# Dilated and latent attention: the sum of a value product's two halves, and the masked product of the row sums, on GpSimd

## The chip, the cores and the metric

One core of a Trainium2 chip runs the whole program. The metric is device microseconds (us) of one execution. PE is TensorE, DVE is VectorE, ACT is ScalarE, POOL is GpSimd, SP is SyncE, which issues the DMAs.

## The reference

Two layers of an encoder, in float32, on a sequence of 1024 rows of 1024 numbers. Only the first layer's attention matters here. It has 8 heads of dilated windows (A) and 8 heads of latent attention (B), 64 wide each:

```python
# A: three windowed branches per head, mixed by the softmax of their log sums
p = jnp.exp(s - m); den = jnp.sum(p, -1)
o = jnp.einsum('bgnhqk,bgnkhd->bgnqhd', p, vw) / den
wts = jax.nn.softmax(jnp.stack(lses, 0), axis=0)
o = jnp.sum(wts[..., None] * jnp.stack(outs, 0), 0)
# B: plain softmax attention over all 1024 keys
s = jnp.einsum('bqhd,bkhd->bhqk', qblk, k) * scale
o = jnp.einsum('bhqk,bkhd->bqhd', jax.nn.softmax(s, -1), v)
```

The result of A and B, side by side, goes through one output projection; then come a feed-forward layer and the second layer.

## The kernel before

Products are made of two parts each, a rounded one and its rest (names that end in h and l), so that TensorE's fast float mode keeps float32's accuracy. A value tile V holds both parts of a head's 64 values side by side in 128 columns. The product of the weights with V therefore gives two half sums, one in PSUM partitions 0 to 63 and one in 64 to 127; they must be added. `halves` does that: ACT copies the half that lies in the wrong partitions out of PSUM into a temporary tile in SBUF (L790), and DVE adds the temporary to the other half, still in PSUM, into the destination (L792). The destination is `S_["s1"]` (the tile mixA), `S_["s2"]` (a part of the tile bX) or `S_["sB"]` (mixB). The temporaries are two tiles taken in turn: `hv` and another part of bX. The PSUM tile `m` has two buffers, shared with all other small products; `b`, for scores and transposes, has three.

Heads come in four pairs. A pair has 8 units of A (4 for each head: `part` 0 or 1, `g` 0 or 1) and 16 of B, and each unit passes three stages that are delayed against each other, so that several units are under way at once: scores (L735 for A, L83 to L85 for B), row minimum on DVE (L738, L823) and exponential on ACT (L745, L825); transposes on PE (L753, L830), whose result is split on ACT and DVE (L74 and L75: aPh and aPl, bPh and bPl); the product with V (L774, L846) and `halves`. `halves` runs after each unit of A and after every fourth unit of B, 48 times in this stage. The second layer's attention uses `halves` too, 16 times.

When a head starts, GpSimd copies its queries and keys in another order: aQ at L712, aK at L713, with one buffer each, so that these copies wait for the last product that reads the old ones. `pair_finish` ends a pair while the next one is under way: the row sums `st` are multiplied by a mask (fXe, L867) and brought into another order by a product; the factors are made; each result is multiplied by them (L922), and GpSimd adds s2 to s1 (L926, two instructions).

Each engine runs its instructions in the order that was fixed when the program was built, and waits in it for semaphores. That order is made by a scheduler from the whole program, so a change of some instructions can move others.

Of the kernel before, what the change touches and what calls it, by code (L numbers as in the profile page):

```python
# [9 lines left out]
AF = mybir.ActivationFunctionType  # L10
ALU = mybir.AluOpType
# [3 lines left out]
P = 128  # L15
# [17 lines left out]
class K:  # L33
# [665 lines left out]
    def dil_unit(self, S_, h, part, g):  # L699
        nc, wk, ps = self.nc, self.wk, self.ps  # L700
        hd = h % 2
        self.pair_state(S_)
        if ("a", h) not in S_:
            S_["a", h] = self.dil_load(h)
        Q, Kt, Bt, V1, V2 = S_["a", h]
        cls = "p l (j c) -> p l c j"
        Kc = S_.get(("k", h), Kt.rearrange(cls, c=4))
        Qc = S_.get(("q", h), Q.rearrange("p (j c) -> p c j", c=4))
        if self.inside and ("k", h) not in S_:
            Kc = S_["k", h] = self.t(wk, [P, 2, 4, 256], F32R, "aK", bufs=1)  # L710
            Qc = S_["q", h] = self.t(wk, [P, 4, 256], F32R, "aQ", bufs=1)
            nc.gpsimd.tensor_copy(Qc, Q.rearrange("p (j c) -> p c j", c=4))  # L712
            nc.gpsimd.tensor_copy(Kc, Kt.rearrange(cls, c=4))  # L713
        st = S_["A"]
        sp = self.t(ps, [P, 4, 256], F32, "b")
        sb = self.t(self.pHA, [P, 4, 256], F32, "aS", bufs=3)
        tiles, biases = [], []
        for tt in range(4):
            j0, j1 = 0, 256
            if part == 0:  # L720
                t = 4 * g + tt
                j0 = 64 if t == 0 else 0
                j1 = 192 if t == 7 else 256
                q = Q[:, t * P:(t + 1) * P]
                k = [Kt[:, l, 128 * t - 64 + j0:128 * t - 64 + j1] for l in range(2)]
                b0 = 64
            else:
                c, hf = 2 * g + tt // 2, tt % 2
                t = 4 * hf + c
                q = Qc[:, c, hf * P:(hf + 1) * P]  # L730
                k = [Kc[:, l, c] for l in range(2)]
                b0 = 128 - 128 * hf
            tiles.append((tt, t, j0, j1))
            for l in range(2):
                nc.tensor.matmul(sp[:, tt, j0:j1], lhsT=q, rhs=k[l], start=l == 0, stop=l == 1)  # L735
            biases.append(Bt[:, part, b0 + j0:b0 + j1])
        for (tt, t, j0, j1), bias in zip(tiles, biases):
            nc.vector.tensor_tensor_reduce(sb[:, tt, j0:j1], sp[:, tt, j0:j1], bias, 1.0, 3e38,  # L738
                                           ALU.add, ALU.min, st[:, part, 0, hd, t:t + 1])
            if j0 > 0:  # L740
                nc.gpsimd.memset(sb[:, tt, :j0], 0.0)
            if j1 < 256:
                nc.gpsimd.memset(sb[:, tt, j1:], 0.0)
        for tt, t, j0, j1 in tiles:
            nc.scalar.activation(sb[:, tt, j0:j1], sb[:, tt, j0:j1], AF.Exp, scale=-1.0,  # L745
                                 bias=st[:, part, 0, hd, t:t + 1], accum_out=st[:, part, 1, hd, t:t + 1])
        yield
        wk, ps = self.wk, self.ps
        tp = self.t(ps, [P, 8, P], F32, "b")
        for tt in range(4):  # L750
            for kc in range(2):
                pos = tt * 2 + kc if part == 0 else (tt // 2) * 4 + kc * 2 + tt % 2
                nc.tensor.transpose(tp[:, pos], sb[:, tt, kc * P:(kc + 1) * P], self.ident)  # L753
        pt = (self.t(wk, [P, 8, P], F32R, "aPh"), self.t(wk, [P, 8, P], F32R, "aPl"))
        self.split(pt[0], pt[1], tp)
        yield
        self.pair_sums(S_, h // 2)
        pv = self.t(ps, [P, 512], F32, "m", bufs=2)
        mms = []
        if part == 0:  # L760
            t0 = 4 * g
            for p0, n, ch in ((1, 2, t0), (5, 2, t0 + 2), (3, 2, t0 + 1), (0, 1, (t0 - 1) % 8), (7, 1, t0 + 3)):
                c0 = (p0 // 2) * P
                mms.append((pv[:, c0:c0 + n * P], V1[:, ch], slice(p0, p0 + n)))
        else:
            for cc in range(2):
                for kc in range(2):
                    p0 = cc * 4 + kc * 2
                    mms.append((pv[:, cc * 256:(cc + 1) * 256], V2[:, kc, 2 * g + cc], slice(p0, p0 + 2)))
        for i, (o, v, pp) in enumerate(mms):  # L770
            for l in range(2):
                first = (i == 0 if part == 0 else i % 2 == 0) and l == 0
                last = (i == 4 if part == 0 else i % 2 == 1) and l == 1
                nc.tensor.matmul(o, lhsT=v, rhs=pt[l][:, pp], start=first, stop=last)  # L774
        if part == 0:
            self.halves(S_["s1"][g], pv, hd)
        else:
            self.halves(S_["s2"][:, g * 512:(g + 1) * 512], pv, hd)
        yield

    def halves(self, dst, pv, hd):

        nc = self.nc
        mine, other = slice(64 * hd, 64 * hd + 64), slice(64 - 64 * hd, 128 - 64 * hd)
        if self.hv:
            self.hv.append(self.hv.pop(0))
            tmp = self.hv[0]
        else:
            tmp = self.t(self.wk, [P, 512], F32, "hv", bufs=2)
        nc.scalar.activation(tmp[mine], pv[other], AF.Copy)  # L790
        o, a, b = dst[mine], pv[mine], tmp[mine]
        nc.vector.tensor_tensor(o, a, b, ALU.add)  # L792

    def mla_load(self, wk, h):
        nc = self.nc
# [13 lines left out]
    def mla_unit(self, S_, h, t):  # L809
        nc, wk, ps = self.nc, self.wk, self.ps  # L810
        hd = h % 2
        self.pair_state(S_)
        if ("b", h) not in S_:
            S_["b", h] = self.mla_load(self.pHB, h)
        Q, Kt, V = S_["b", h]
        st = S_["B"]
        sp = self.t(ps, [P, S], F32, "b")
        q = [Q[:96, l, t * P:(t + 1) * P] for l in range(2)]
        for half in range(2):
            ks = slice(half * 512, half * 512 + 512)  # L820
            self.mm3(sp[:, ks], q, [Kt[:96, l, ks] for l in range(2)], True, True)
        pr = self.t(wk, [P, S], F32, "bP", bufs=3)
        nc.vector.tensor_tensor_reduce(pr, sp, self.zero.to_broadcast([P, S]), 1.0, 3e38, ALU.add, ALU.min,  # L823
                                       st[:, 0, hd, t:t + 1])
        nc.scalar.activation(pr, pr, AF.Exp, scale=-1.0, bias=st[:, 0, hd, t:t + 1],  # L825
                             accum_out=st[:, 1, hd, t:t + 1])
        yield
        tp = self.t(ps, [P, KC, P], F32, "b")
        for kc in range(KC):
            nc.tensor.transpose(tp[:, kc], pr[:, kc * P:(kc + 1) * P], self.ident)  # L830
        if t % 2 == 0:
            S_["pt"] = (self.t(self.pHB, [P, KC, 256], F32R, "bPh"), self.t(self.pHB, [P, KC, 256], F32R, "bPl"))
        pt = S_["pt"]
        xs = slice((t % 2) * P, (t % 2 + 1) * P)
        self.split(pt[0][:, :, xs], pt[1][:, :, xs], tp, eng=nc.gpsimd if t in () else None)
        yield
        if t % 2 == 0:
            yield
            return
        if t % 4 == 1:  # L840
            S_["pv"] = self.t(ps, [P, 512], F32, "m", bufs=2)
        pv = S_["pv"]
        o = pv[:, (t % 4 // 2) * 256:(t % 4 // 2) * 256 + 256]
        for kc in range(KC):
            for l in range(2):
                nc.tensor.matmul(o, lhsT=V[:, kc], rhs=pt[l][:, kc], start=(kc == 0 and l == 0),  # L846
                                 stop=(kc == KC - 1 and l == 1))
        if t % 4 == 3:
            self.pair_sums(S_, h // 2)
            self.halves(S_["sB"][t // 4], pv, hd)  # L850
        yield

    def pair_finish(self, S_, j, mixT, parts=(0, 1, 2)):

        T = {}
        nc = self.nc
        tt_ = nc.vector.tensor_tensor

        def gather():
# [4 lines left out]
            st = S_["A"]  # L864
            Xe = self.t(wk, [P, 4, 32], F32, "fXe", bufs=1)
            s1 = st[:, 1].rearrange("p q h t -> p (q h t)")
            tt_(Xe, s1.unsqueeze(1).to_broadcast([P, 4, 32]), self.mask4.unsqueeze(2).to_broadcast([P, 4, 32]), ALU.mult)  # L867
            pc = self.t(ps, [P, 512], F32, "m", bufs=2)
            Xv = Xe.rearrange("p a (x c) -> p (a x) c", c=4)
            for c in range(4):  # L870
# [39 lines left out]
        def apply():  # L910
# [18 lines left out]
            yield  # L929

        return [gather(), factors(), apply()]

    def pool(self, name, bufs=1, side=None, space=None):
# [1078 lines left out]
```

## Time and profile before

| | us |
|---|---|
| median of 3 runs | 2456.16 |
| lowest and highest | 2453.56, 2458.27 |
| the profiled execution's own time | 2455.98 |
| its span, first to last instruction | 2454.2 |

The profile is of one execution. Busy time of PE is a share of the span in which some matmul was under way; matmuls overlap, so that a short gap between them may not show as idle time. The stage in question lies between 326 and 655 us of the span.

### The profile page before, as it was taken

What the parts mean: (1) busy time and instruction counts of PE and PEld (TensorE: products, weight loads), DVE (VectorE), ACT (ScalarE), POOL (GpSimd) and SP (SyncE); (2) the same over time, 40 slices, a digit from 0 to 9 for tenths busy, and PEclk for the clock granted to TensorE, in tenths of its full rate; (3) what the DMA queues carried; (4) which work ended last, traced back from release to release, by engine and by line L of the source; (5) the groups of instructions that cost most, each with busy time, mean ns of one, the idle gap of its engine ahead of it and who ended that gap; (6) DMA issues with size and microseconds to landing.
All of it is one profiled execution on the core that took longest, in us unless ns stands there. A gap on an engine that the chain in (4) does not pass through costs nothing. (4 is left out here: it accounts for less than half of the span.)

```text
span 2454.2 us, 31655 instructions
## 1 busy us (share of the span) xinstructions
PE 2396.1 (98%) x12218; PEld 2021.0 (82%) x12218; DVE 1704.1 (69%) x2175; ACT 1238.6 (50%) x1912; POOL 234.6 (10%) x233
## 2 busy tenths in 40 slices
PE   9999999999999999999999999999999999999998
PEld 7887888888787888888888898977778888888887
DVE  6676578989758666665885685876687656657854
ACT  6553377888456443442334754375665344333332
POOL 1111112121020000000000200242210000000002
PEclk9999999999999999999999999999999999999999
DMA  7456877552252332234844445599533223139331
GB/s 259 167 193 207 280 171 165 122 133 73 100 206 69 103 103 78 78 103 162 288 129 156 141 158 166 135 210 215 182 103 103 75 80 103 52 128 330 121 116 69
DMA packets 206678, 357.83 MB, mean 146 GB/s; under 512 B 13512, under 2 KB 123304, under 8 KB 206272
## 3 DMA queue, kind: packets, MB, share of 16 engines
q1 hardware_dynamic: 206528, 355.81, 46.7%
q8 instruction: 97, 1.59, 0.3%
q14 instruction: 53, 0.43, 0.1%
HBM read 258.83 MB, written 105.32 MB: 148 GB/s over the span
## 5 line engine op out<-in xcount | busy, mean ns | idle before, releaser
L1815 DVE TENSOR_TENSOR u<-u,b 128x1024 f32<-128x1024 f32 (+1 forms) x119 | 141.2, 1205 | 125.7 <-PE b L85 125.7
L1721 ACT ACTIVATE raw<-raw,gains 128x512 f32<-128x512 f32 (+1 forms) x248 | 162.0, 707 | 120.3 <-DMA raw<-in_ffn_w_gu_dram 83.3
L74 ACT ACTIVATE wh<-sr 128x1024 fp32r<-128x1024 f32 (+1 forms) x121 | 125.2, 1042 | 190.8 <-PE b L84 176.6
L75 DVE TENSOR_TENSOR wl<-sr,wh 128x1024 fp32r<-128x1024 f32 (+1 forms) x121 | 146.3, 1216 | 99.0 <-ACT wh L74 98.9
L84 PE MATMUL b<-B1l,wh 128*128 128x512 f32 x440 | 172.5, 392 | 2.2 <-DVE B1l L75 2.2
L83 PE MATMUL b<-B1h,wh 128*128 128x512 f32 x440 | 172.6, 392 | 1.8 <-ACT B1h L74 1.8
L85 PE MATMUL b<-B1h,wl 128*128 128x512 f32 x440 | 172.1, 391 | 0.0
L74 ACT ACTIVATE wh<-raw 128x1024 fp32r<-128x1024 f32 (+1 forms) x94 | 97.8, 1050 | 137.7 <-PE b L84 119.4
L75 POOL TENSOR_TENSOR ml<-msrc,mh 128x512 fp32r<-128x512 f32 x16 | 21.0, 1320 | 1212.9 <-ACT mh L74 1209.1
L75 DVE TENSOR_TENSOR wl<-raw,wh 128x1024 fp32r<-128x1024 f32 (+1 forms) x94 | 115.4, 1233 | 29.7 <-ACT wh L74 29.3
L83 PE MATMUL b<-wh,wh 128*128 128x512 f32 x336 | 130.7, 389 | 0.0
L84 PE MATMUL b<-wl,wh 128*128 128x512 f32 x336 | 130.7, 389 | 0.0
L85 PE MATMUL b<-wh,wl 128*128 128x512 f32 x336 | 130.7, 389 | 0.0
L83 PE MATMUL b<-wh,mh 128*128 128x512 f32 x320 | 127.1, 397 | 0.6 <-DVE mixB L922 0.4
L85 PE MATMUL b<-wh,ml 128*128 128x512 f32 x320 | 125.5, 392 | 0.4 <-POOL ml L75 0.4
L84 PE MATMUL b<-wl,mh 128*128 128x512 f32 x320 | 125.3, 392 | 0.0
L84 PEld LDWEIGHTS b<-B1l,wh 128*128 128x128 f32 x440 | 83.0, 189 | 20.2 <-DVE B1l L75 2.8
L83 PEld LDWEIGHTS b<-B1h,wh 128*128 128x128 f32 x440 | 82.9, 188 | 19.9 <-ACT B1h L74 2.6
L85 PEld LDWEIGHTS b<-B1h,wl 128*128 128x128 f32 x440 | 83.0, 189 | 17.6
L75 DVE TENSOR_TENSOR bPl<-b,bPh 128x1024 fp32r<-128x1024 f32 x64 | 78.0, 1221 | 10.9 <-ACT bPh L74 10.1
L825 ACT ACTIVATE bP<-bP,stB 128x1024 f32<-128x1024 f32 x64 | 73.4, 1147 | 20.5 <-DVE stB L823 19.5
L823 DVE CUSTOM_DVE_ANT_0 bP<-b,zero 128x1024 f32<-128x1024 f32 x64 | 77.9, 1218 | 5.9 <-PE b L85 3.2
(652 smaller groups left out, 7096.4 us busy)
## 6 DMA issues: line engine op xcount, KB each, us to landing
raw<-in_ffn_w_gu_dram SPq DMA_DIRECT2D x88, 512.0 KB, 4.6
hS<-hid SPq DMA_DIRECT2D x44, 512.0 KB, 3.2
st<-hS SPq DMA_DIRECT2D x32, 512.0 KB, 5.1
xt<-xp SPq DMA_DIRECT2D x24, 512.0 KB, 3.8
x<-xt SPq DMA_DIRECT2D x24, 512.0 KB, 3.2
raw<-in_od_w_in_dram SPq DMA_DIRECT2D x20, 512.0 KB, 4.3
raw<-kS SPq DMA_DIRECT2D x16, 512.0 KB, 7.1
raw<-in_ev_w_in_dram SPq DMA_DIRECT2D x14, 512.0 KB, 7.0
```

The source lines that it names most:

```text
L74: nc.scalar.activation(hi, src, AF.Copy)
L75: (eng or nc.vector).tensor_tensor(lo, src, hi.bitcast(F32), ALU.subtract)
L83: mm(ps, lhsT=l[0], rhs=r[0], start=start, stop=False, skip_group_check=more)
L84: mm(ps, lhsT=l[0], rhs=r[1], start=False, stop=False, skip_group_check=more)
L85: mm(ps, lhsT=l[1], rhs=r[0], start=False, stop=stop, skip_group_check=more)
L823: nc.vector.tensor_tensor_reduce(pr, sp, self.zero.to_broadcast([P, S]), 1.0, 3e38, ALU.add, ALU.min, st[:, 0, hd, t:t + 1])
L825: nc.scalar.activation(pr, pr, AF.Exp, scale=-1.0, bias=st[:, 0, hd, t:t + 1], accum_out=st[:, 1, hd, t:t + 1])
L1721: k.nc.scalar.activation(r[:, :self.nb, a], r[:, :self.nb, a], AF.Copy, scale=self.g[:, half * 4 + a:half * 4 + a + 1])
L1815: add = lambda o, x: k.nc.vector.tensor_tensor(o, x, pb, ALU.add)
```

## The change

`halves` gets a switch. With it, ACT copies both half sums out of PSUM, the second one straight into the destination, and GpSimd adds the temporary to the destination in SBUF. The switch is on for all 32 calls of A and for the 14 calls of B of the heads 0 to 6; the two of head 7 and the second layer's 16 stay as they are. The masked product fXe goes from DVE to GpSimd, 4 times. (The program of the change has the instruction of L867 at L871, and of L926 at L930; its new lines are L793 and L794.)

```diff
         if part == 0:
-            self.halves(S_["s1"][g], pv, hd)
+            self.halves(S_["s1"][g], pv, hd, True)
         else:
-            self.halves(S_["s2"][:, g * 512:(g + 1) * 512], pv, hd)
+            self.halves(S_["s2"][:, g * 512:(g + 1) * 512], pv, hd, True)
...
-    def halves(self, dst, pv, hd):
+    def halves(self, dst, pv, hd, pool=False):
...
         nc.scalar.activation(tmp[mine], pv[other], AF.Copy)
         o, a, b = dst[mine], pv[mine], tmp[mine]
-        nc.vector.tensor_tensor(o, a, b, ALU.add)
+        if pool:
+            nc.scalar.activation(o, a, AF.Copy)
+            nc.gpsimd.tensor_tensor(o, o, b, ALU.add)
+        else:
+            nc.vector.tensor_tensor(o, a, b, ALU.add)
...
         if t % 4 == 3:
-            self.halves(S_["sB"][t // 4], pv, hd)
+            self.halves(S_["sB"][t // 4], pv, hd, h < 7)
...
-            tt_(Xe, s1.unsqueeze(1).to_broadcast([P, 4, 32]), self.mask4.unsqueeze(2).to_broadcast([P, 4, 32]), ALU.mult)
+            nc.gpsimd.tensor_tensor(Xe, s1.unsqueeze(1).to_broadcast([P, 4, 32]), self.mask4.unsqueeze(2).to_broadcast([P, 4, 32]), ALU.mult)
```

How the order on the engines changes is shown at two places. First, GpSimd where a pair ends and the next begins (418 us of the span for the first pair). Before, the copies aQ and aK and the two additions of L926 are followed by clearing the edges of the score tile aS:

```order
L712 COPY aQ_3839<-wh_3823 128x1024 [waits DMAHW5_49,PE_49,Pool_49]
L713 COPY aK_3838<-raw_3824 128x2048 [waits DMAHW6_49,Pool_49]
L926 TENSOR_TENSOR mixA_2557<-mixA_2557,bX_2280 128x512 [waits DVE_49]
L926 TENSOR_TENSOR mixA_2557<-mixA_2557,bX_2280 128x512
L741 MEMSET aS_3843 128x64 [waits Activation_49]
```

With the change, the same place reads:

```order
L712 COPY aQ_3855<-wh_3839 128x1024 [waits DMAHW5_49,PE_49]
L713 COPY aK_3854<-raw_3840 128x2048 [waits DMAHW6_49]
L930 TENSOR_TENSOR mixA_2557<-mixA_2557,bX_2280 128x512 [waits DVE_49]
L930 TENSOR_TENSOR mixA_2557<-mixA_2557,bX_2280 128x512
L741 MEMSET aS_3859 128x64 [waits Activation_49]
L794 TENSOR_TENSOR mixA_2557<-mixA_2557,hv_2564 64x512 [waits Activation_49]
L794 TENSOR_TENSOR bX_2280<-bX_2280 64x512 [waits Activation_49]
L794 TENSOR_TENSOR mixB_2553<-mixB_2553,hv_2564 64x512 [waits Activation_49]
```

The new additions stand behind the copies and L926 in GpSimd's queue. ACT at the same place, before (aPh and bPh are splits of A's and B's weights, bP the exponential of B):

```order
L790 ACTIVATE hv_2564<-m_3641 64x512 [waits PE_49]
L745 ACTIVATE aS_3710,stA_3310<-aS_3710,stA_3310 128x256 [waits DVE_49]
L74 ACTIVATE aPh_3736<-b_3727 128x1024
L790 ACTIVATE hv_2564<-m_3549 64x512 [waits DVE_49]
L790 ACTIVATE bX_2280<-m_3698 64x512 [waits PE_49]
```

And with the change:

```order
L790 ACTIVATE hv_2564<-m_3653 64x512 [waits PE_49]
L793 ACTIVATE mixA_2557<-m_3653 64x512
L745 ACTIVATE aS_3724,stA_3320<-aS_3724,stA_3320 128x256 [waits DVE_49]
L74 ACTIVATE aPh_3750<-b_3741 128x1024
L790 ACTIVATE bX_2280<-m_3711 64x512 [waits PE_49]
L793 ACTIVATE bX_2280<-m_3711 64x512 [waits Pool_49]
L790 ACTIVATE hv_2564<-m_3561 64x512 [waits Pool_49]
L793 ACTIVATE mixB_2553<-m_3561 64x512
L829 ACTIVATE bP_3780,stB_3321<-bP_3780,stB_3321 128x1024 [waits DVE_49]
L74 ACTIVATE bPh_3707<-b_3783 128x8x128 [waits PE_49]
```

ACT now waits for GpSimd twice there, and an exponential and a split stand behind these waits; before, it waited for DVE. The second place is ACT some 27 us later (451 us of the span). Before, the split aPh stands ahead of four exponentials of A:

```order
L790 ACTIVATE hv_2564<-m_4039 64x512 [waits PE_49]
L74 ACTIVATE aPh_4080<-b_4071 128x1024 [waits PE_49]
L745 ACTIVATE aS_4053,stA_3310<-aS_4053,stA_3310 128x256 [waits DVE_49] x3
L745 ACTIVATE aS_4053,stA_3310<-aS_4053,stA_3310 128x192 [waits DVE_49]
L74 ACTIVATE bPh_4035<-b_4111 128x8x128 [waits PE_49]
```

With the change it stands behind them:

```order
L790 ACTIVATE hv_2564<-m_4057 64x512 [waits PE_49]
L793 ACTIVATE mixA_2557<-m_4057 64x512
L745 ACTIVATE aS_4072,stA_3320<-aS_4072,stA_3320 128x256 [waits DVE_49] x3
L745 ACTIVATE aS_4072,stA_3320<-aS_4072,stA_3320 128x192 [waits DVE_49]
L74 ACTIVATE aPh_4099<-b_4090 128x1024 [waits PE_49]
L74 ACTIVATE bPh_4053<-b_4130 128x8x128 [waits PE_49]
```

The split aPh has moved behind the four exponentials. It does so at two or three such places of each pair.

## Rows read from the trace of the kernel before

**Rows 1.** The page's head.

```profile
span 2454.2 us, 31655 instructions
```

**Rows 2.** Windows: the whole stage.

```profile
core 0: us, PE busy (x) PEld busy (x) DVE busy (x) ACT busy (x) POOL busy (x), PEclk, DMA share, GB/s
326.00:655.00 329.00, 313.06 (x2189) 280.62 (x2188) 296.60 (x579) 256.92 (x505) 56.69 (x35) 0.99 0.52 123
```

**Rows 3.** What PE waited for, 320 to 660 us: total us, times, longest.

```profile
PE b L753 <- DVE bPl L75: 2.3, 6, 0.5
PE b L735 <- DVE stB L823: 2.1, 5, 0.5
PE m L774 <- DVE mixA L792: 1.7, 1, 1.7
PE b L830 <- DVE aPl L75: 1.5, 1, 1.5
```

**Rows 4.** Timeline of POOL at pair ends: start, us, instruction, idle before it.

```profile
418.71 2.11 POOL L712 CAST aQ<-wh 128x1024 fp32r<-128x1024 f32 x1 [30.91 <-PE b L735]
420.74 3.96 POOL L713 CAST aK<-raw 128x2048 fp32r<-128x2048 f32 x1
424.61 3.13 POOL L926 TENSOR_TENSOR mixA<-mixA,bX 128x512 f32<-128x512 f32 x2
...
589.63 4.04 POOL L926 TENSOR_TENSOR mixA<-mixA,bX 128x512 f32<-128x512 f32 x2
```

**Rows 5.** A DVE add of halves (ns, lowest/median/highest); POOL's subtraction (page's groups).

```profile
L792 DVE TENSOR_TENSOR mixA<-m,hv x10: 672/689/695, 328.1 to 623.7; 64x512 f32<-64x512 f32 x10
...
L75 POOL TENSOR_TENSOR ml<-msrc,mh 128x512 fp32r<-128x512 f32 x16 | 21.0, 1320 | 1212.9 <-ACT mh L74 1209.1
```

**Rows 6.** Timeline of ACT at the first pair's end and 27 us later.

```profile
425.58 0.58 ACT L790 ACTIVATE bX<-m 64x512 f32<-64x512 f32 x1
426.06 1.15 ACT L825 ACTIVATE bP<-bP,stB 128x1024 f32<-128x1024 f32 x1
...
427.32 1.95 ACT L74 ACTIVATE bPh<-b 128x1024 fp32r<-128x1024 f32 x2
...
451.28 1.03 ACT L74 ACTIVATE aPh<-b 128x1024 fp32r<-128x1024 f32 x1
452.48 0.51 ACT L745 ACTIVATE aS<-aS,stA 128x256 f32<-128x256 f32 x1 [0.17 <-DVE stA L738]
...
453.98 0.44 ACT L745 ACTIVATE aS<-aS,stA 128x192 f32<-128x192 f32 x1
```

**Rows 7.** Timeline of DVE at the first and the third pair's end.

```profile
427.77 0.68 DVE L792 TENSOR_TENSOR bX<-m,bX 64x512 f32<-64x512 f32 x1 [1.27 <-POOL mixA L926]
...
430.12 2.34 DVE L75 TENSOR_TENSOR bPl<-b,bPh 128x1024 fp32r<-128x1024 f32 x2
...
587.27 3.47 DVE L75 TENSOR_TENSOR wl<-raw,wh 128x1024 fp32r<-128x1024 f32 x1
```

**Rows 8.** Timeline of PE at the first and the third pair's end.

```profile
431.39 1.09 PE L753 MATMUL b<-ident,aS 128*128 128x128 f32 x8
...
591.39 0.38 PE L774 MATMUL m<-aPh,wl 128*128 128x256 f32 x1 [1.67 <-DVE mixA L792]
...
597.14 0.33 PE L846 MATMUL m<-bPh,bV 128*128 128x256 f32 x1
```

**Rows 9.** The masked product (ns); POOL and PE beside the second one (timeline).

```profile
L867 DVE TENSOR_TENSOR fXe<-stA,mask x4: 293/2268/2273, 381.0 to 616.7; 128x128 f32<-128x128 f32 x4
...
461.59 3.96 POOL L713 CAST aK<-raw 128x2048 fp32r<-128x2048 f32 x1
...
463.44 2.27 DVE L867 TENSOR_TENSOR fXe<-stA,mask 128x128 f32<-128x128 f32 x1 [0.18 <-ACT aS L745]
...
466.91 0.50 PE L83 MATMUL b<-bK,bQ 96*128 96x512 f32 x1 [0.46 <-DVE stB L823]
```

**Rows 10.** Windows: the stretch after PE's wait at 591.39 us; granted clock third from the end.

```profile
592.93:596.34 3.41, 3.41 (x18) 3.41 (x18) 3.13 (x6) 2.79 (x5) 0.83 (x2) 0.50 0.00 0
```

## The prediction

> **What bounds the kernel now.** I read the head of the page first: the span is 2454.2 us [rows 1], the execution's own time 2455.98, so 1.8 us lie around the span. That time is 0.18 us under the median of the three runs, 2456.16, so sums made on this profile can be set against the median as they are. About 0.2%, 4.9 us, is what a measurement of this kernel can tell from no change.
>
> Then the windows, for the stage that the change touches (326 to 655 us). Of its 329 us PE is busy 313.06, DVE 296.60, ACT 256.92 and POOL 56.69 [rows 2]. So PE sets the end here, though DVE (90%) and ACT (78%) are close behind it; taking work from DVE is worth only what PE now waits for DVE. The waits give that: the largest that the change can touch are 2.3 us on bPl, 2.1 on stB, 1.7 on mixA and 1.5 on aPl [rows 3], 7.6 us in all. With the smaller ones that the view lists below these, I put the most that can be gained at 11 us (an estimate). The 31.7 us of additions that leave DVE, 46 of 0.689 us [rows 5], are therefore no measure of the gain.
>
> Last the timelines where PE does wait. They lie where GpSimd is busy. At the end of each of the first three pairs (418.71 us for the first, 501 and 584 for the others) it has aQ, aK and L926 in a row, and ends L926 at 424.61 + 3.13 = 427.74 [rows 4]. Beside that DVE's addition into bX waits 1.27 us for L926 [rows 7].
>
> **The change part by part.**
>
> *The work itself.* DVE loses 46 × 0.689 = 31.7 us and four masked products. ACT gains 46 copies like the one of 0.58 us into bX [rows 6], 26.7 us, and goes to 284 of 329 us, 86%, still under PE. GpSimd gains 46 additions of two operands in SBUF. Before shows no such addition of 64x512 there; the bounds are its 128x512 subtraction, 1.320 us [rows 5], and half of L926's pair, 3.13 / 2 = 1.57 [rows 4]. I take 1.32, that row being the nearest in what is read and written: 61 us, so that GpSimd goes to about 118 of 329 us. No engine becomes the bound by its sum. What counts is who waits behind whom.
>
> The Trainium skill ("GPSIMD Engine Reference", section Performance versus the Vector engine) speaks against the change: elementwise work belongs on VectorE, since GpSimd takes 1.96 times as long for an addition. By it an addition would take 0.689 × 1.96 = 1.35 us, an estimate, which would move term A below by 0.03 us at each place; the row gives 1.32.
>
> *Term A, the ends of pairs: a loss.* The new additions stand in GpSimd's queue behind aQ, aK and L926, and ACT waits for two of these. The copy into bX (L793) must wait for L926, which reads bX, as DVE's addition did. The next copy, into hv, waits for the addition that reads hv's old contents, the first one behind L926. That is new, and what stands behind it on ACT is the copy into mixB, an exponential and the split bPh, on which DVE's bPl and then PE's L753 depend (L753 needs the score buffer that bPl gives back). By times of the first pair: L926 ends at 427.74, the addition of 1.32 ends at 429.1, hv and mixB take about 0.5 each (start to start in [rows 6], 425.58 to 426.06), to 430.1; the exponential 1.15, to 431.3; the first bPh half of 1.95, to 432.3; bPl half of 2.34 [rows 7], to 433.5. PE's L753 then starts at 433.6 and not at 431.39 [rows 8]: +2.2 us. The second pair has the same pattern. At the third L926 ends at 589.63 + 4.04 = 593.67 [rows 4]; the addition ends at 595.0, hv and mixB at 596.1, the exponential at 597.25, bPh at 598.25, and PE's product with bPh starts at 598.3 and not at 597.14 [rows 8]: +1.2. The 1.67 us that PE waits at 591.39 for DVE's mixA would go, but that is ahead of this later wait, which takes it back. Sum A: 2.2 + 2.2 + 1.2 = +5.6. Bounds: 0, if the additions start earlier than I have it (rival 2), and 5.6 + 3 × 0.25 = 6.4 with additions of 1.57.
>
> *Term B, the order on ACT: a loss.* At two or three places of a pair the split aPh now stands behind four exponentials of A. Before, it started at 451.28, and the exponentials ran from 452.48 to 453.98 + 0.44 [rows 6]. They wait for DVE's row minimum; so aPh, ready at 451.3, is held up to 3 us, and with it aPl and the transposes' PSUM buffer. PE has three such buffers and other units under way, which hide most of it. Nine places at 0 to 1.0 us (what is left of those 3 us when the other two buffers each cover one product block of about 1 us, such as L753's 1.09 [rows 8]); PE waited for aPl 1.5 us only once in the stage [rows 3], so I take 0.4: +3.6, bounds 0 to 9.
>
> *Term C, the masked product: a gain.* On DVE it took 2.27 us in the first three pairs, beside GpSimd's copy aK (461.59 to 465.55), and 0.293 at best [rows 9]. Behind it DVE's stB is late, and PE waits 0.46 us at 466.91 [rows 9] and soon after once more, on bPl. On GpSimd the product lies behind aK and one addition, about 1.5 us later than now, but PE's product with it comes only some 12 us later in the order, so this costs nothing; without that cover it would cost these 1.5 us three times. I count 0.63 and 0.47 us from start to start of PE's products at the two waits, 1.1 in all: 3 × 1.1 = −3.3.
>
> *Term D, the clock: a loss.* After PE's wait of 1.67 us at 591.39 the granted clock fell to 0.50, 1.2 of 2.4 GHz, from 592.93 to 596.34 [rows 8, 10]; 3.41 us at half clock are 1.7 us of lost work. The new waits of term A, some 2.9 us with the gap that is there now, could do the same at the first two ends: 0 to 2 × 1.7 = 3.4. I take +2.0.
>
> *Term E, the rest.* PE's wait for aPl in the last pair (1.5 us [rows 3]) ends on a DVE that has now less ahead of it: −1.0, bounds 0 to −1.5. The other additions taken from DVE cost or gain nothing, as PE's queue holds other units' products beside them.
>
> Sum: +5.6 + 3.6 − 3.3 + 2.0 − 1.0 = +6.9, 2455.98 + 6.9 = 2462.9, **2463 us**.
>
> **The rivals.**
>
> *1: no change that can be told.* B and D cost nothing: the other units under way hide the late aPh, and the clock stays up. 5.6 − 3.3 − 1.0 = +1.3, 2457 us. For it speaks that PE has three score buffers; against it, that the clock did fall after a wait shorter than the new ones. Chance 0.28.
>
> *2: faster.* The wait at the ends of pairs is no longer than today's. It decides whether the addition that ACT waits for ends by 426.9 us in the first pair, 2.2 us ahead of my 429.1: it would if the copies aQ and aK started that much earlier, or if DVE, freed of its additions, brought the factors' products forward. Then A, B and D are nil, and the waits on DVE fall away: −3.3 − 1.0 to the whole 11, taken −7, 2449 us (2445 to 2452). Against it: aQ waits for PE's last product with the old aQ, 30.91 us of idle time [rows 4], so GpSimd can't begin earlier than PE does. Chance 0.16.
>
> *3: slower still, by contention.* GpSimd's 61 us of additions would slow those DVE operations that read both operands from SBUF, as fXe was slowed from 0.293 to 2.27 [rows 9] and the split wl from half of bPl's 2.34 to 3.47 beside L926 [rows 7]. Operations that read PSUM weren't: mixA's additions stay within 0.672 and 0.695 [rows 5]. Four splits wl at up to 2.3 us more each are 9.2: 2463 + 9 = 2472 us. The Trainium skill (the same page, section Specifications) has GpSimd share its SBUF interfaces with VectorE, with contention for DVE instructions with two SBUF inputs; the two rows agree, 2.27 beside 0.293. Against it: only one of the four wl lies beside GpSimd today, and after the change most additions lie beside DVE work on PSUM. Chance 0.06.
>
> The forecast itself, slower by terms A to E, has 0.50, its own range 2458 to 2469 (B and D at nothing or near their upper bounds).
>
> **How the numbers follow.** Faster than 2451.3: most of rival 2 (0.15) and a tail of rival 1 (0.02), 0.17. Slower than 2461.1: rival 3 (0.06), of the forecast 0.44 and of rival 1 0.03, 0.53. Within 0.2%: the rest, 0.30. As rivals on both sides hold a third of the chance, the range reaches from 2448, which takes in most of rival 2, to 2472; some 0.15 is left out, split between the two sides.
>
> **What the profile after would show.** Term A: on ACT, before the copy into hv, a wait for POOL's first addition that ends near 429, 512 and 595 us (shifted by what came earlier), and PE's wait at L753 on bPl grown from under half a us to 2 to 3 us. GpSimd's additions at 1.3 us. Term B: waits of PE for aPl, or of L753 or L735 for aPl's buffer, at 451 us and its like. Term C: no fXe on DVE, and no wait of PE at 466.91's place. Term D: the granted clock at 0.5 for 3 us after the first and second end. The forecast is wrong if PE's gap there is no longer than today's, or if additions take far under 1.32 us, since half of the loss rests on that one queue.

## The result, and the profile after

| | before | after |
|---|---|---|
| median, us | 2457.22 (6 runs, 2451.97 to 2461.37) | 2472.95 (6 runs, 2471.61 to 2475.40) |
| span of the profiled execution, us | 2454.2 | 2470.3 |

The ratio is 1.0069, 95% interval 1.0058 to 1.0079: 16.9 us slower (14.2 to 19.4); the two medians themselves lie 15.7 apart. The forecast was 2463, slower by 6.9 us, with a range up to 2472. Sign and places were right; the size was less than half of what came.

The windows of the kernel after say that no engine became the bound. The first row is the stage (326 to 671 us now; see [rows 2] for before), the second the stretch behind PE's longest new wait. Columns as in [rows 2]; granted clock third from the end.

```profile
326.00:671.00 345.00, 317.93 (x2186) 283.24 (x2184) 259.91 (x529) 281.78 (x550) 117.66 (x85) 0.98 0.49 118
433.86:437.28 3.42, 2.81 (x13) 2.81 (x14) 2.88 (x9) 3.38 (x8) 0.79 (x1) 0.50 0.95 185
```

DVE went from 296.6 to 259.9 us, ACT from 256.9 to 281.8, POOL from 56.7 to 117.7, nearly the sums forecast. PE is busy for about what it was and the stage is 16 us longer: the time went into waits. What PE waited for, 320 to 680 us of the kernel after (total us, times, longest; its L827 and L834 are L823 and L830 of before):

```profile
PE b L753 <- DVE bPl L75: 8.4, 7, 2.9
PE b L83 <- DVE aPl L75: 5.5, 7, 1.2
PE b L834 <- DVE aPl L75: 2.6, 3, 0.9
PE b L735 <- DVE stB L827: 2.5, 5, 0.8
```

Against [rows 3], the waits for bPl grew from 2.3 to 8.4 us, with one of 2.9 among them, and those for aPl are now 8.1 us. Both are waits for DVE, which has less to do than before; so the cause lies ahead of DVE. The first kind: GpSimd at the place of [rows 4] (timeline: start, us, instruction, idle before it and what ended it).

```profile
419.56 2.08 POOL L712 CAST aQ<-wh 128x1024 fp32r<-128x1024 f32 x1 [19.66 <-PE b L735]
421.59 3.94 POOL L713 CAST aK<-raw 128x2048 fp32r<-128x2048 f32 x1
425.45 3.12 POOL L930 TENSOR_TENSOR mixA<-mixA,bX 128x512 f32<-128x512 f32 x2
428.49 0.17 POOL L741 MEMSET aS<- 128x64 f32 x1
428.59 1.30 POOL L794 TENSOR_TENSOR mixA<-mixA,hv 64x512 f32<-64x512 f32 x1
```

ACT beside it:

```profile
428.60 0.59 ACT L793 ACTIVATE bX<-m 64x512 f32<-64x512 f32 x1 [1.52 <-POOL mixA L930]
429.92 0.59 ACT L790 ACTIVATE hv<-m 64x512 f32<-64x512 f32 x1 [0.73 <-POOL mixA L794]
430.53 0.59 ACT L793 ACTIVATE mixB<-m 64x512 f32<-64x512 f32 x1
431.02 1.14 ACT L829 ACTIVATE bP<-bP,stB 128x1024 f32<-128x1024 f32 x1
432.15 1.00 ACT L74 ACTIVATE bPh<-b 128x1024 fp32r<-128x1024 f32 x1
```

DVE, and then PE:

```profile
433.19 1.23 DVE L75 TENSOR_TENSOR bPl<-b,bPh 128x1024 fp32r<-128x1024 f32 x1 [3.52 <-ACT bPh L74]
```

```profile
430.45 1.15 PE L735 MATMUL b<-raw,wh 128*128 128x192 f32 x8
434.47 1.76 PE L753 MATMUL b<-ident,aS 128*128 128x128 f32 x7 [2.87 <-DVE bPl L75]
```

This is the chain of term A, link by link: L926 (L930 here) ends at 428.5, the addition at 429.9, hv, mixB, exponential and bPh follow on ACT, bPl ends at 434.4, and PE's L753 starts 2.87 us after PE had run out of work. The rows start 0.85 us later than before, so that the forecast 433.6 is 434.45 here; it came at 434.47. Towards the end of the wait the granted clock fell to 0.50, 1.2 GHz, and stayed there from 433.86 to 437.28 (second row of the windows). Before, this stretch had none. The second place repeats all this (a wait of 2.87 us, then half clock from 522.5 us). At the third, PE waits 1.60 us for bPh and 0.97 for bPl, with half clock from 611.5 us.

The second kind: ACT at the first of this pair's three late splits. (The place of [rows 6], 451.28 us before, is the second, now at 459.06. The one shown here stood ahead of its four exponentials before, at 441.83.)

```profile
446.69 0.50 ACT L745 ACTIVATE aS<-aS,stA 128x256 f32<-128x256 f32 x1
...
448.18 0.49 ACT L745 ACTIVATE aS<-aS,stA 128x256 f32<-128x256 f32 x1
448.67 1.00 ACT L74 ACTIVATE aPh<-b 128x1024 fp32r<-128x1024 f32 x1
```

The split aPh starts only when the four exponentials are through. DVE idles for it, and PE's next product for B waits for the score buffer that aPl gives back. The three rows of PE are the three late splits:

```profile
449.70 1.22 DVE L75 TENSOR_TENSOR aPl<-b,aPh 128x1024 fp32r<-128x1024 f32 x1 [2.65 <-ACT aPh L74]
```

```profile
450.98 0.50 PE L83 MATMUL b<-bK,bQ 96*128 96x512 f32 x1 [0.64 <-DVE aPl L75]
...
461.39 0.50 PE L83 MATMUL b<-bK,bQ 96*128 96x512 f32 x1 [0.87 <-DVE aPl L75]
...
472.02 1.09 PE L834 MATMUL b<-ident,bP 128*128 128x128 f32 x8 [0.87 <-DVE aPl L75]
```

The last of the three stands where the masked product had cost two waits in [rows 9].

For most kernels below I read the same seven distances from POOL's timeline: from the start of one copy aQ to that of the next, and from the last to the last L926 (us; the sum is the stage but for its ends). A's places, where L926 meets the first head of the next pair, lie in distances 3, 5 and 7, together with two late splits each in 3 and 5; the masked product lies in 2, 4, 6 and 7, with one late split each in 2, 4 and 6 (and one each in 1 and 7). The first distance differed by up to 0.9 us between kernels that have the same order in it, so that only the sum of larger differences is read from it.

| kernel | 1 | 2 | 3 | 4 | 5 | 6 | 7 | sum |
|---|---|---|---|---|---|---|---|---|
| before | 40.91 | 41.62 | 40.83 | 41.62 | 40.87 | 41.62 | 61.7 | 309.2 |
| after | 41.89 | 41.44 | 46.38 | 41.51 | 46.65 | 41.48 | 66.6 | 326.0 |
| fxe_only | 40.87 | 40.27 | 40.86 | 40.27 | 40.90 | 40.29 | 61.0 | 304.5 |
| boundary_only | 40.52 | 41.60 | 44.59 | 41.63 | 44.29 | 41.64 | 64.7 | 319.0 |
| late_aph | 40.73 | 41.62 | 42.62 | 43.22 | 42.64 | 43.22 | 62.0 | 316.0 |
| halves_only | 41.94 | 44.49 | 46.42 | 42.90 | 47.65 | 44.46 | 68.3 | 336.2 |
| boundary_dve | 41.85 | 41.45 | 42.89 | 41.47 | 42.86 | 41.64 | 62.1 | 314.3 |
| pinned | 40.00 | 40.32 | 43.13 | 40.31 | 44.66 | 40.31 | 65.9 | 314.6 |
| pinned_boundary | 39.86 | 40.29 | 40.88 | 40.29 | 40.88 | 40.41 | 62.1 | 304.7 |
| first_dve | 40.72 | 40.27 | 41.21 | 40.32 | 41.19 | 40.30 | 63.0 | 307.0 |
| two_dve | 40.26 | 40.29 | 40.30 | 40.30 | 40.21 | 40.29 | 62.1 | 303.8 |

The stage lost 16.8 us, the whole span 16.1; 5.5, 5.8 and 4.9 us of it in the three distances with A's places.

### The profile page after: what moved, and what is told of

It reads as the page before. It is cut to its first block, busy times and chain, and to the rows that moved or that the text cites. A ratio compares the mean times of both kernels' runs of the same rounds, so it can differ in the third digit from the quotient of the medians.

```text
span 2470.3 us, 31735 instructions
## 1 busy us (share of the span) xinstructions
PE 2400.1 (97%) x12218; PEld 2024.0 (82%) x12218; DVE 1667.6 (68%) x2125; ACT 1262.4 (51%) x1958; POOL 295.2 (12%) x283
## 5 line engine op out<-in xcount | busy, mean ns | idle before, releaser
L827 DVE CUSTOM_DVE_ANT_0 bP<-b,zero 128x1024 f32<-128x1024 f32 x64 | 78.0, 1219 | 20.2 <-PE b L85 17.3
L829 ACT ACTIVATE bP<-bP,stB 128x1024 f32<-128x1024 f32 x64 | 73.3, 1145 | 12.3 <-DVE stB L827 11.4
```

## The experiments

Theory Q: the loss comes from queues, at a few places: ACT waits there for GpSimd (A), splits aPh stand late (B), and the masked product is a gain (C). Rival L: every moved instruction costs a little on its new engine, about 0.35 us in each of 46 calls. Each edit below is against the kernel named; an ordering edge adds no instruction, it only makes the scheduler put one behind another.

### One part at a time, on the kernel before

**fxe_only**: the masked product alone.

```diff
-            tt_(Xe, s1.unsqueeze(1)...
+            nc.gpsimd.tensor_tensor(Xe, s1.unsqueeze(1)...
```

> The kernel before with the masked product alone on GpSimd; the order on every engine is otherwise that of before. Theory Q (queues: the change loses at a few places where ACT waits for GpSimd or a split stands late, and the masked product alone is a gain as in term C): -3.3 us, 2453 to 2454 against 2457, PE's waits at 383.7, 466.2 and 548.7 us gone. Rival L (load: every moved instruction costs a little on the fuller engine): 0 to +1.

Measured: 2452.86 us against 2455.44, ratio 0.9991 (0.9982 to 0.9999); the stage 4.7 us shorter, 1.35 in each of distances 2, 4 and 6. On GpSimd the product takes 0.42 us, while it took DVE 2.27 [rows 9]. C is real: 4.0 us in these three distances, where 3.3 were forecast. The other 0.7 us lie in distance 7 and can't be the product's, which took DVE only 0.29 us there before. One thing that differs there is the clock: before, PE's wait of 1.67 us at 591.39 had half clock behind it [rows 8, 10]. Here the same wait has none (PE, then the windows; granted clock third from the end):

```profile
588.75 0.39 PE L774 MATMUL m<-aPh,wl 128*128 128x256 f32 x1 [1.63 <-DVE mixA L792]
```

```profile
588.75:600.00 11.25, 10.45 (x80) 9.80 (x81) 10.86 (x26) 10.50 (x25) 2.52 (x4) 1.00 0.01 2
```

**elsewhere**: nine calls of halves on ACT and GpSimd, where no addition stands behind L926.

```diff
-            self.halves(S_["s1"][g], pv, hd)
+            self.halves(S_["s1"][g], pv, hd, h in (1, 3, 5) and g == 1)
...
-            self.halves(S_["s2"][:, g * 512:(g + 1) * 512], pv, hd)
+            self.halves(S_["s2"][:, g * 512:(g + 1) * 512], pv, hd, h in (1, 3, 5) and g == 1)
...
-            self.halves(S_["sB"][t // 4], pv, hd)
+            self.halves(S_["sB"][t // 4], pv, hd, h in (1, 3, 5) and t == 7)
```

> The kernel before with nine of the 46 calls on ACT and GpSimd, none of them behind L926 (heads 1, 3 and 5: second call of each part of A, second call of B); the order on every engine is otherwise that of before. Theory Q: 0 (-1 to +1), since no wait changes place. Rival L, the loss of 16 us spread over 46 calls: 9 x 0.35 = +3.1 us.

Measured: 2455.72 against 2455.44, ratio 0.9999 (0.9991 to 1.0008). PE's four largest waits inside the stage are those of before, to a tenth of a us. Rival L's 3.1 us lie outside the interval (up to 2.0).

**boundary_only**: nine other calls, those behind L926.

```diff
-            self.halves(S_["s1"][g], pv, hd)
+            self.halves(S_["s1"][g], pv, hd, h in (2, 4, 6) and g == 0)
...
-            self.halves(S_["sB"][t // 4], pv, hd)
+            self.halves(S_["sB"][t // 4], pv, hd, h in (2, 4, 6) and t == 3)
```

(The call for s2 has the condition of s1; one ordering edge holds a split where it was.)

> The kernel before with another nine calls on ACT and GpSimd: those whose additions stand behind L926 in GpSimd's queue (heads 2, 4 and 6: first call of each part of A, first call of B). Theory Q: the stall of 2.9 us of PE at L753 appears at each of the three places, net of today's waits 2.1 each, and the granted clock falls to 0.5 for 3.4 us at the first two (1.7 us each): 3 x 2.1 + 2 x 1.7 = +9.7 us (7 to 12). Rival L: 9 x 0.35 = +3.1, no new wait.

Measured: 2468.41, ratio 1.0057 (1.0045 to 1.0069); the stage is 9.8 us longer, in distances 3, 5 and 7 alone: 3.8, 3.4 and 3.0 (the time rose by 13, just over the 12 that I had allowed; what is over lies outside the stage, where the span differs by 1.4 us already ahead of the first aQ, 337.6 against 336.2, and was not followed). What PE waited for, 320 to 680 us (L759 here is L753):

```profile
PE b L759 <- DVE bPl L76: 9.0, 9, 2.9
```

The stall of 2.9 us came at two of the three places. At the third PE waits 1.62 us for bPh and 0.96 for bPl, and half clock follows (PE, then the windows; L857 is L846 of before):

```profile
606.41 0.39 PE L857 MATMUL m<-bPh,bV 128*128 128x256 f32 x1 [1.62 <-ACT bPh L75]
607.76 1.06 PE L759 MATMUL b<-ident,aS 128*128 128x128 f32 x8 [0.96 <-DVE bPl L76]
```

```profile
609.00:612.40 3.40, 3.40 (x16) 3.29 (x16) 2.95 (x3) 3.35 (x10) 0.04 (x1) 0.52 0.00 0
```

The same number of calls as in elsewhere, at another place: 10 us and not 0. This decides against L.

**late_aph**: no work moved; ordering edges put seven splits behind the exponentials, as in the change.

```diff
+            for k, n in [(13, 52), (14, 56), (15, 60), (21, 84), (22, 88), (23, 92), (28, 116)]:
+              for n in range(n, n + 4):
+                  self.tc.add_manual_dep(self.pins[0][k - 1], self.pins[1][n].name, mybir.DependencyInfo(
+                    mybir.DependencyClass.NoSync, mybir.DependencyReason.DATA), reason="pin")
```

(pins holds the splits aPh and the exponentials of A in the order of the code.)

> The kernel before, nothing moved between engines; an ordering edge alone puts seven splits aPh behind the four exponentials of A that they preceded, as the change has them (three places each in the second and the third pair, one in the last). Theory Q: PE waits 0.9 and 1.0 us for aPl at two places of each of the two pairs, and up to 1.1 at the third, beside 0 to 1 in the last pair: +5 us (3.9 to 7). Rival L: 0, for no engine has more to do.

Measured: 2462.90, ratio 1.0037 (1.0024 to 1.0049); the stage 6.8 us longer, 1.8 in each of distances 3 and 5 and 1.6 in each of 4 and 6. The stage stays within the 7 us that I had allowed, the time, 7.5 over before, is just above them. The order of ACT alone costs this, with the same work everywhere: B is real, about 1 us for a late split and more than twice what I had taken. In distances 4 and 6 the wait that grew is one for stB, behind the masked product, which is on DVE in this kernel:

```profile
469.65 1.09 PE L837 MATMUL b<-ident,bP 128*128 128x128 f32 x8 [2.19 <-DVE stB L830]
```

So a late split costs 0.9 us by itself (distances 3 and 5), and 1.6 where the masked product on DVE keeps another buffer at the same time.

### Taking parts out of the change

**halves_only**: the masked product back on DVE (the diff of fxe_only, reversed).

> The change without its masked product, which is back on DVE; the order on every engine is otherwise that of the change. Theory Q: at the masked product's place the change already has a wait of 1.14 us for aPl where before had two of 0.63 and 0.47, so that part C's gain is hidden behind part B's wait or adds to it: 0 to +3.3 us over the change, 2473 to 2476. Rival L: the change minus four small instructions, 2472.

Measured: 2482.17, ratio to before 1.0109 (1.0096 to 1.0122): 9.2 us over the change's median, three times the most that I expected. DVE at the masked product's place, and PE (timelines):

```profile
381.83 2.37 DVE L871 TENSOR_TENSOR fXe<-stA,mask 128x128 f32<-128x128 f32 x1 [1.99 <-ACT aS L745]
384.12 1.21 DVE L75 TENSOR_TENSOR aPl<-b,aPh 128x1024 fp32r<-128x1024 f32 x1
```

```profile
385.39 1.70 PE L834 MATMUL b<-ident,bP 128*128 128x128 f32 x8 [2.10 <-DVE aPl L75]
```

Here the masked product stands ahead of the split aPl that is late already, and PE waits for both: 2.10 us where the change waits 0.9. So in the change's order C and B meet in one wait. This wait comes three times. In distance 4 it costs 1.4 us over the change; in 2 and 6, where half clock follows it, 3.0. Windows behind the first two:

```profile
385.70:389.10 3.40, 3.40 (x18) 3.40 (x16) 2.77 (x4) 1.91 (x2) 1.26 (x1) 0.50 1.04 169
475.00:478.40 3.40, 2.06 (x18) 2.06 (x19) 3.40 (x5) 1.89 (x2) 2.70 (x3) 1.00 1.07 214
```

So some 3 of the 9.2 us are the clock's. Whether GpSimd's additions make the product dearer is asked by pinned_halves below.

**boundary_dve**: the change, but the nine calls of boundary_only stay on DVE (the conditions of boundary_only reversed, with edges for two splits).

> The change, but the nine calls whose additions stand behind L926 (heads 2, 4 and 6: first call of each part of A, first call of B) add on DVE as before, and two splits are held where the change has them. Theory Q: the three stalls at L753 and the slow clock behind them go, 9 to 11 us less than the change: 2462 to 2464. Rival L: 9 x 0.35 = 3.1 less, 2470.

Measured: 2464.89, ratio to before 1.0037 (1.0025 to 1.0049), 8.1 us under the change (9 to 11 expected); the stage 11.7 us shorter than the change's. Distances 3 and 5 keep 2.0 us over before: the two late splits in each.

**pinned**: the change, with edges that put nine splits ahead of the exponentials again.

```diff
+            for k, n in [(6, 24), (7, 28), (13, 52), (14, 56), (15, 60), (21, 84), (22, 88), (23, 92), (28, 116)]:
+              for n in range(n, n + 4):
+                  self.tc.add_manual_dep(self.pins[1][n], self.pins[0][k - 1].name, ...
```

> The change with ordering edges that put nine splits aPh ahead of the four exponentials of A again, as before. Theory Q: the waits for aPl go, about 2 us in each of the second and third pair, 1 in the last, 1 in the first, and the masked product's gain of up to 1.1 per pair comes out: 5 to 9 us less than the change, 2464 to 2468. Rival L: no less, 2472 to 2473.

Measured: 2461.75, ratio to before 1.0022 (1.0013 to 1.0032), 11.2 us under the change, more than the 5 to 9 expected; the stage 11.4 us shorter. Distances 2, 4 and 6 are now those of fxe_only: with the split in time the masked product's gain comes out. Distances 3 and 5 have A alone, and show the clock by itself: both have the wait of 2.9 us at L753, and only the second a slow stretch behind it. PE and the windows of pinned around the two:

```profile
433.69 1.09 PE L759 MATMUL b<-ident,aS 128*128 128x128 f32 x8 [2.90 <-DVE bPl L76]
517.12 1.81 PE L759 MATMUL b<-ident,aS 128*128 128x128 f32 x8 [2.90 <-DVE bPl L76]
```

```profile
517.33:520.75 3.42, 3.42 (x18) 3.42 (x17) 2.56 (x9) 3.38 (x8) 1.37 (x2) 0.50 0.60 132
428.00:436.00 8.00, 5.10 (x43) 4.67 (x42) 3.91 (x9) 7.22 (x14) 3.89 (x4) 1.00 0.97 186
```

43.13 against 44.66 us: A without the clock is 43.13 − 40.83 = 2.3 us, the clock another 1.5. The change has the slow stretch at both places, so 1.3 of the 11.4 us that pinned gains (3.25 in distance 3 against 1.99 in 5) is the clock's and not the splits'.

**pinned_boundary**: both edits, with edges for three more splits.

> Both of these edits together: 37 calls on ACT and GpSimd, nine on DVE, splits ahead of the exponentials as before, the masked product on GpSimd. Theory Q: what is left is part C and the few small waits for DVE: 2452 to 2456, 1 to 5 us under the kernel before. Rival L: 37 x 0.35 = 13 us over the kernel before, 2470.

Measured: 2452.80 against 2456.05, ratio 0.9995 (0.9986 to 1.0003). With A and B out, 37 calls on ACT and GpSimd cost nothing: the stage is 304.7 us, fxe_only's is 304.5.

### The links of A, and the price of the masked product

**pinned_halves**: pinned, with the masked product on DVE.

> The kernel pinned with the masked product back on DVE. Theory S (halves_only lost 9 us because the masked product stood ahead of a split aPl that was late already): without the late split the product costs what it costs in the kernel before, 4 to 5 us over pinned, 2465 to 2467. Rival N (GpSimd's additions beside it make it dearer): 9 to 10 us over pinned, 2471 to 2472, and a product of over 2.4 us.

Measured: 2465.77, 4.0 us over pinned: the size that theory S gave, and against N. The traces make the product cheaper than S has it: 0.8 us in each of distances 2, 4 and 6, not 1.35, while another 1.6 lie in distance 3, where half clock follows the wait here and not in pinned. On DVE the four products take 1.25 us in the mean, less than in the kernel before (1.78). POOL and DVE beside the first one (timelines):

```profile
377.90 4.03 POOL L718 CAST aK<-raw 128x2048 fp32r<-128x2048 f32 x1
```

```profile
380.47 1.60 DVE L878 TENSOR_TENSOR fXe<-stA,mask 128x128 f32<-128x128 f32 x1 [0.74 <-ACT aS L750]
```

The copy ends at 381.93 and the product at 382.07. In [rows 9] they end at 465.55 and 465.71. The product ends 0.15 us behind the copy both times; it is shorter here because it began later.

**pinned_finish**: pinned, with L926 on DVE and edges for five more splits.

```diff
-                    nc.gpsimd.tensor_tensor(mixT[0][:, j, g * 512:(g + 1) * 512].rearrange(jc, c=4),
+                    nc.vector.tensor_tensor(mixT[0][:, j, g * 512:(g + 1) * 512].rearrange(jc, c=4),
```

> The kernel pinned with the eight additions of L926 on DVE in place of GpSimd, so that nothing but the two copies aQ and aK stands ahead of the first addition of halves at the three places; all 46 calls stay on ACT and GpSimd. Theory Q (the stall is the length of GpSimd's queue, of which L926 is 3.1 us): the additions end 3 us earlier, PE's stall of 2.9 us at L753 falls under 0.7 and the slow clock behind it goes: 6 to 9 us less than pinned, 2453 to 2456, up to 3 more if DVE's added work shows. Rival D (the stall comes from ACT's doubled copies at this place): the stall stays over 2 us, 2460 to 2463.

Measured: 2477.70, ratio to before 1.0087 (1.0073 to 1.0101): 16 us over pinned, and neither theory. The wait at L753 did shrink, to 1.0 at most, but a new one came. DVE, PE and POOL of this kernel at the first place (timelines; L937 is L926):

```profile
417.65 3.87 POOL L718 CAST aK<-raw 128x2048 fp32r<-128x2048 f32 x1
...
417.87 6.58 DVE L937 TENSOR_TENSOR mixA<-mixA,bX 128x512 f32<-128x512 f32 x2
...
425.97 1.30 PE L841 MATMUL b<-ident,bP 128*128 128x128 f32 x5 [4.99 <-DVE stA L743]
```

The two additions need 6.58 us on DVE beside GpSimd's copy and the addition behind it, and 2.05 in the last pair, where GpSimd rests:

```profile
661.98 2.05 DVE L937 TENSOR_TENSOR mixA<-mixA,bX 128x512 f32<-128x512 f32 x2
```

Everything behind them on DVE, a row minimum first, is late, and PE waits 4.99 us three times. The experiment can't speak on A, since it moved the places against each other; the next two do.

**first_dve**: pinned, but the call whose addition is first behind L926 stays on DVE.

```diff
-            self.halves(S_["s1"][g], pv, hd, True)
+            self.halves(S_["s1"][g], pv, hd, h not in (2, 4, 6) or g == 1)
```

> The kernel pinned, but the one call whose addition stands first behind L926 (first part of A, first call, heads 2, 4 and 6) adds on DVE. In the order ACT then copies into hv and mixB ahead of its wait for L926, and waits for GpSimd only with the copy into bX. Theory Q: of the stall of 2.9 us at L753 what goes is the wait of 0.7 for the addition and the two copies of 0.6 that stood behind it, 1.9 us; 0.9 to 1.0 stay, the slow clock goes, 3 x 1.9 + 1.5 x 2 = 8.7 us less than pinned: 2452 to 2455. Rival W (it is the wait for L926, which went from DVE to ACT, that holds PE): the stall stays over 2 us, 2459 to 2462.

Measured: 2454.93 against 2456.13, ratio 0.9997 (0.9989 to 1.0006). One wait of ACT for GpSimd is left, for L926; PE's wait at L753 is 1.33 us, where 0.9 to 1.0 were expected (ACT and PE, timelines of this kernel):

```profile
429.61 0.59 ACT L800 ACTIVATE bX<-m 64x512 f32<-64x512 f32 x1 [0.77 <-POOL mixA L937]
```

```profile
433.56 1.09 PE L759 MATMUL b<-ident,aS 128*128 128x128 f32 x8 [1.33 <-DVE bPl L76]
```

Distances 3 and 5 are 0.3 to 0.4 over before and no slow clock follows: rival W falls. The larger part of A, 1.9 of its 2.3 us, is the second wait, for hv's addition, with the copies that stand behind it.

**two_dve**: the call for s2 there on DVE too (the same condition on the line of s2, edges for two more splits).

> The same, and the call of the second part of A there also on DVE, so that ACT waits for GpSimd at none of the three places; the call of B there stays on ACT and GpSimd. Both theories: the stall at L753 is that of the kernel before, under 0.5 us; 9 to 11 us less than pinned, 2451 to 2454. If it stays above 2457, neither wait of ACT for GpSimd is the cause.

Measured: 2452.85 against 2456.13, ratio 0.9986 (0.9978 to 0.9995). ACT waits for GpSimd at none of the places, distances 3 and 5 are 40.3 and 40.2, under those of before. With fxe_only, this is the fastest: 0.1% under the kernel before, and 0.8% under the change.

## Why the prediction was wrong in size

**What bounds the kernel: right.** The 31.7 us that left DVE gained nothing that shows: two_dve and fxe_only differ by 40 calls on GpSimd and by 0.7 us of the stage.

**Term A: right in place and links, small in size.** Forecast +2.2, +2.2 and +1.2. pinned gives 2.3 for the first (43.13 − 40.83), and the second is like it but for the clock; boundary_only gives 3.0 for the third (64.7 − 61.7). There the chain itself came as forecast: PE's product with bPh starts at 606.41, and 598.3 plus 8.16 us, by which aQ starts later there than before, is 606.46. The other 1.8 us lie behind it. I listed no wait at L753 there (0.96 us), and the slow stretch that lay ahead of this product before [rows 10] now lies behind it. 2.3 + 2.3 + 3.0 = 7.6 against 5.6.

**Term B: the step that failed.** "PE has three such buffers and other units under way, which hide most of it": they don't. I took 0.4 for each of nine places, 3.6 in all. boundary_dve, which keeps the late splits and leaves out A, is 5.1 us of the stage over before with C's −4.0 in it: 9.1 for the nine splits (1.0 of it in the first distance, where kernels differ by as much without a cause). Between the change and pinned the stage differs by 11.4 us, 10.1 without the clock; late_aph, where nothing else is changed, has 6.8 for seven places. So about 1 us a split, the upper end of the bounds of 0 to 1.0. The rows show why: DVE idled 2.65 us for aPh and PE's next B product needed the buffer that the late aPl held. My argument that PE waited for aPl only once in the kernel before [rows 3] was no evidence, as the splits stood in time there; nor was it quite so, for the same view lists two more such waits, one of them inside the stage:

```profile
PE b L83 <- DVE aPl L75: 1.4, 2, 0.7
```

**Term C: right, and outweighed.** −3.3 forecast, −4.0 in distances 2, 4 and 6 of fxe_only. In the change these are only 0.1 to 0.2 under before, since a late split stands in each and costs 1.2 (after less pinned). The gain is there, and B takes it back.

**Term D: about right, by a weak argument.** +2.0 forecast for the first two places. boundary_only's distances 3, 5 and 7 are 10.1 longer, which leaves 10.1 − 7.6 = 2.5, and 1.5 is what one slow stretch cost in pinned. But I had inferred it from a single wait, at 591.39 [rows 8], and in fxe_only that same wait has full clock behind it. **Term E: nothing** came of its −1.0: pinned_boundary's stage is fxe_only's.

Sum of the stage by the experiments: A and D +10.1 (boundary_only), B +9.1 (boundary_dve), C −4.0 (fxe_only): +15.2, where the stage lost 16.8. The other 1.6 us no experiment assigns. Of the 9.9 us that the forecast was short, 5.5 lie in B, 2.0 in A, 1.0 in E and 0.5 in D; C gave 0.7 more than I had counted.

**The rivals.** The additions ended at 429.9, which is 429.05 without the shift of 0.85, not by 426.9 (rival 2). Contention (rival 3) was not the cause: all GpSimd's additions but the nine cost nothing, and DVE's splits wl took 7.1 us in all, as before. Its mechanism exists, though: pinned_finish shows it. The rule cited there, of the Trainium skill ("GPSIMD Engine Reference", section Specifications), on DVE instructions with two SBUF inputs agrees with that trace: 6.58 us beside the copy, 2.05 alone.

## What to carry to other kernels

When work goes from one in-order engine to two others, price the waits that change engine, not the busy time: nine calls cost 10 us at one place and another nine nothing elsewhere, because an exponential and a split stood behind ACT's new wait. And read what a scheduler does with the rest: here about 9 of the 17 us came from splits that no line of the diff touches, and a few ordering edges gave them back. The number of buffers did not tell the slack here; whether PE waits for the instruction that is moved late is seen by moving it alone.

## What was not expected of the hardware

A masked product of 128x128 that took DVE 2.27 us beside GpSimd's copy takes GpSimd itself 0.40 to 0.44 us. GpSimd is the slower engine for it (DVE alone took 0.29), and yet five times faster there. On DVE its length is set by when it begins: in before, late_aph, halves_only and pinned_halves it ends 0.14 to 0.16 us behind the end of GpSimd's copy aK, after 1.6 to 2.4 us.

In these traces the length of a wait of PE does not tell whether half clock follows. That of 2.9 us was followed by 3.4 us at 1.2 GHz at one place of pinned and by none at another, with the same instructions around. In halves_only two of three waits of 2.1 us were followed by it; the 1.67 us of before were, the same wait of 1.63 us in fxe_only was not, nor were the 1.33 us of first_dve.
